# Second block's latent-only adaLN vectors: from TensorE chunks to GpSimd products and ScalarE sums

## The chip, the cores and the metric

One core of one Trainium2 chip runs the whole program in one launch. The metric is the device time in microseconds (us) of that launch; less is better. Engines are named as the profile names them: PE is TensorE's matmuls, DVE is VectorE, ACT is ScalarE, POOL is GpSimd, SP is the queue that issues most transfers. Line numbers (L169) are those of the kernel before; where a line of the changed kernel is meant, the text says so.

## What is computed

Two blocks of a flow-matching backbone, for 256 context tokens and 256 latent tokens of width 1024, and a final norm. Cut to what the change touches:

```python
for layer in range(2):
    mod_l = silu(c) @ mod_w[layer] + mod_b[layer]        # c: (1, 1024), mod_w[layer]: (1024, 6144)
    mod_c = silu(c_ctx) @ mod_w[layer] + mod_b[layer]
    sh1l, sc1l, g1l, sh2l, sc2l, g2l = split(mod_l, 6)   # vectors of 1024
    sh1c, sc1c, g1c, sh2c, sc2c, g2c = split(mod_c, 6)
    # mixer on rmsnorm(x, g) * (1 + sc1) + sh1, added to x with gate g1
    # feed-forward on rmsnorm(x, g') * (1 + sc2) + sh2, added to x with gate g2
    # in the last layer the context takes part in the mixer's input alone
```

So of the second block's six vectors the context needs only the first two (sh1, sc1); the other four (g1, sh2, sc2, g2) are needed for the latent tokens alone.

## The kernel before

The stages follow each other: first block's mixer, first feed-forward (`conv_ffn` with l = 0, 512 tokens), second mixer, second feed-forward (l = 1, 256 tokens). Activations lie transposed, features on partitions. Every large product is made of three matmuls of split operands (L180 to L182): a weight block is copied by ACT into a rounded upper part `wh` (L168), and the rest `wl` = raw - `wh` is made by DVE or POOL (L169). A `Stream` does that: `load` (L154) fetches 16 blocks of 128x128, `split` makes one unit of 8 blocks (128x1024), `get` splits one unit ahead, and a load may also call one function of a list `fill`. `wh` and `wl` have four buffers each, the fetched `raw` two.

The first feed-forward: eleven column pairs j in a first half, eleven in a second. For each pair two products of eight blocks with 512 columns (24 matmuls each, into banks `gps` and `mps`), ACT scales the result (`y`, L823), DVE adds the eight other taps of the convolution (L829), ACT applies silu (L890), POOL multiplies (L893), ACT rounds (`mh`, L896) and POOL makes the rest (`ml`, L897). The up-weights' `wl` are POOL's; each pair uses one load, so two units. The first four products (units of loads 0 and 1) run together. After the eleven pairs come 88 blocks of the down-weights (`dn`), whose first units are POOL's too.

`mod_chunk(l, j)` computes 512 entries of `mod_l` and `mod_c`: two transfers of 1 MB, eight matmuls of 512 columns (L239) with silu(c) as a 128x32 operand, a copy by ACT (L256), four transposes (L259), a sum and bias by DVE (L263 to L267) into `mod` columns (`comps`). Of the second block's twelve chunks, chunk 2 stands ahead of the first feed-forward's norm, nine (3, 0, 1, 4, 5, 8, 9, 6, 7) are its `fill`, one at each load from the third on, chunk 10 stands ahead of the second feed-forward's norm and chunk 11 is its `fill`.

Ahead of each feed-forward stands a norm: `Norm.add(k)` squares the k-th of eight tiles of x on ACT (L281), adds on DVE (L283), sums over partitions on PE (L127), takes the root on DVE (L112 to L118), spreads it by PE and ACT (L135, L136 `rstd`); then `norm_mod` makes `hh` and `hl` for each k on DVE and ACT (L310, L316, L318).

A scheduler orders every engine's instructions when the program is built: it moves an instruction forward where its engine is free and its inputs are there by its own estimate, so what stands late in the code can run early. On the chip each engine then works through its list in that order.

Of the kernel before, what the change touches and what calls it, by code (L numbers as in the profile page):

```python
# [9 lines left out]
F32 = mybir.dt.float32  # L10
F32R = mybir.dt.float32r
I32 = mybir.dt.int32
AF = mybir.ActivationFunctionType
ALU = mybir.AluOpType
AX = mybir.AxisListType

P = 128
D = 1024
KD = 8
# [8 lines left out]
FF = 22  # L28
# [23 lines left out]
def block_kernel(ctx: ExitStack, tc: tile.TileContext, A: dict, out: bass.AP):  # L52
    nc = tc.nc
    PSUM = bass.MemoryType.PSUM
    v, s, g, te = nc.vector, nc.scalar, nc.gpsimd, nc.tensor
# [8 lines left out]
    rawp = ctx.enter_context(tc.tile_pool(name="rawp", bufs=2))  # L64
# [9 lines left out]
    def nm(b):  # L74
        _u[0] += 1
        return f"{b}_{_u[0]}"
# [10 lines left out]
    def mps():  # L87
        return psm.tile([P, 512], F32, tag="m", name=nm("mps"))
# [12 lines left out]
    def pc(name, i=0, n=1):  # L101
        o = _off[name] + i
        return prm[:, o:o + n]
# [124 lines left out]
    comps = [[cp.tile([P, KD, 2], F32, tag=f"mod{l}_{i}", name=f"mod{l}_{i}") for i in range(6)] for l in range(2)]  # L228

    def mod_chunk(l, j, pool=rawp, psa=vps, tag="raw", n=2, bufs=None):  # L230

        ps = psa()
        w = KD // n
        for i in range(n):
            raw = pool.tile([P, w * 512], F32, tag=tag, name=nm("rawm"), bufs=bufs)
            nc.sync.dma_start(out=raw, in_=A["modw"][l, j, :, i * w * 512:(i + 1) * w * 512])
            for kk in range(w):
                k = i * w + kk
                te.matmul(out=ps[32 * (k % 4):32 * (k % 4) + 32, :], lhsT=spad[:, k, :], rhs=raw[:, kk * 512:(kk + 1) * 512],  # L239
                          start=k < 4, stop=k >= 4)  # L240
        mod_out(l, 4 * j, 4, ps, psa)
# [11 lines left out]
    def mod_out(l, c, n, ps, psa):  # L253

        ev = t2((P, n * P))
        s.copy(out=ev, in_=ps)  # L256
        pt = psa()[:, :n * P].rearrange("p (a b) -> p a b", b=P)
        for a in range(n):
            te.transpose(pt[:, a, :], ev[:, a * P:(a + 1) * P], ident)  # L259
        col = lambda name, o: pc(name, o, n).unsqueeze(2).to_broadcast([P, n, 2])  # L260
        i, k = c // KD, c % KD
        dst = comps[l][i][:, k:k + n, :]
        v.tensor_reduce(out=dst, in_=pt.rearrange("p a (q c) -> p a c q", q=4)[:, :, 0:2, :], axis=AX.X, op=ALU.add)  # L263
        v.tensor_tensor(out=dst, in0=dst, in1=col("modb", l * 48 + c), op=ALU.add)
        if i in (1, 4):

            v.scalar_tensor_tensor(out=dst, in0=dst, scalar=1.0, in1=col("nmg" if i == 1 else "nfg", l * 8 + k), op0=ALU.add, op1=ALU.mult)  # L267

    accs = np_.tile([P, T], F32, tag="acc", name="acc", bufs=1)

    class Norm:
# [29 lines left out]
    def norm_mod(l, comp_sh, comp_sc, segs, r, between=lambda k, acts: None, tiles=None):  # L301
        c0, c1 = segs[0][1], segs[-1][2]
        hs = [] if tiles is None else tiles
        sh, sc = comps[l][comp_sh], comps[l][comp_sc]
        acts = lambda k: hs[k]
        for k in range(KD):
            between(k, acts)
            y = t2()
            for ci, a, b in segs:
                v.scalar_tensor_tensor(out=y[:, a:b], in0=xT[k][:, a:b], scalar=sc[:, k, ci:ci + 1], in1=r[:, a - c0:b - c0],  # L310
                                       op0=ALU.mult, op1=ALU.mult)
            if tiles is None:
                hs.append(htiles(k))
            h_, l_ = hs[k]
            for ci, a, b in segs:
                s.activation(out=h_[:, a:b], in_=y[:, a:b], func=AF.Identity, bias=sh[:, k, ci:ci + 1])  # L316
            for ci, a, b in segs:
                v.scalar_tensor_tensor(out=l_[:, a:b], in0=y[:, a:b], scalar=sh[:, k, ci:ci + 1], in1=h_[:, a:b].bitcast(F32),  # L318
                                       op0=ALU.add, op1=ALU.subtract)
        return acts  # L320

    def htiles(k):
        return (hp.tile([P, T], F32R, tag=f"hh{k}", name=nm("hh")), hp.tile([P, T], F32R, tag=f"hl{k}", name=nm("hl")))
# [15 lines left out]
    E = Ctx()  # L339
# [11 lines left out]
    with tc.tile_pool(name="stp", bufs=6) as stp:  # L351
# [19 lines left out]

        acts = norm_mod(0, 0, 1, SEGS, r, start)
    fill0 = [lambda j=j: mod_chunk(0, j) for j in (4, 5, 8, 9, 6, 7)]
    fill1 = [lambda j=j: mod_chunk(1, j) for j in (3, 0, 1, 4, 5, 8, 9, 6, 7, 11)]
    E.fill0, E.W0 = fill0, W0
    nrm = Norm(0, T)
    with ExitStack() as st:
# [4 lines left out]
    mod_chunk(1, 2, rawp, mps)  # L382
    acts = norm_mod(0, 3, 4, SEGS, r)
    with ExitStack() as st:
        hs, nrms = [], [Norm(a, b) for _, a, b in SEGS]

        def then(m, sgs):
            for sg in sgs:
                nrms[sg[0]].add(m)
                if m == KD - 1:  # L390
                    hs[:] = hs or [htiles(k) for k in range(KD)]
                    norm_mod(1, 0, 1, (sg,), nrms[sg[0]].row(), tiles=hs)

        conv_ffn(E, st, 0, acts, fill1[:-1], then)
    for k in range(KD):
        dump(f"x2_{k}", xT[k])
    with ExitStack() as st:
# [3 lines left out]
        dump(f"x3_{k}", xT[k])  # L401
    with ExitStack() as st:
        r = nrm.row()
        mod_chunk(1, 10, rawp, mps)
        acts = norm_mod(1, 3, 4, SEGS[1:], r)
        op = st.enter_context(tc.tile_pool(name="outp", bufs=1))
        ot = op.tile([P, 2, D], F32, tag="ot", name="ot")

        def turn(k):

            y = op.tile([P, TL], F32, tag="yt", name=nm("yt"), bufs=2)
            s.activation(out=y, in_=xT[k][:, 256:T], func=AF.Copy, scale=pc("fng", k))
            pt = mps()
            for t in range(2):
                te.transpose(pt[:, t * P:(t + 1) * P], y[:, t * P:(t + 1) * P], ident)
            s.copy(out=ot[:, :, k * P:(k + 1) * P], in_=pt[:, :TL].rearrange("p (t n) -> p t n", n=P))

        nrm = Norm(256, T)

        def then(m, sgs):  # L420
            nrm.add(m)
            if 0 < m < KD - 1:
                turn(m - 1)

        conv_ffn(E, st, 1, acts, fill1[-1:], then)

        r = nrm.cols()
        turn(KD - 2)
        turn(KD - 1)
        for h in range(2):  # L430
            for t in range(2):
                y = ot[:, t, h * 512:(h + 1) * 512]
                if h == 0:
                    v.tensor_scalar(out=y, in0=y, scalar1=r[:, t:t + 1], scalar2=None, op0=ALU.mult)
                else:
                    s.activation(out=y, in_=y, func=AF.Copy, scale=r[:, t:t + 1])
                nc.sync.dma_start(out=out[t, :, h * 512:(h + 1) * 512], in_=y)
# [364 lines left out]
        then(m)  # L802


def conv_ffn(E, st, l, acts, fill, then):
    nc, tc, A = E.nc, E.tc, E.A
    v, s, g = E.v, E.s, E.g
    nm = E.nm
    full = l == 0
    n = T if full else TL  # L810
# [53 lines left out]

    nh = 2 if full else 1
    per = FF // nh
    dn = E.Stream(A[f"dn{l}"], FF * KD, eng=lambda u: g if u * 8 % (per * KD) < per * 4 else v)
    LAG = 4
    for hf in range(nh):
        hm = []  # L870
# [5 lines left out]
        for jj in range(per):  # L876
            j = hf * per + jj
# [312 lines left out]
def layout(inp):  # L1190
    f = {k: np.asarray(a) for k, a in inp.items()}
    A = {}
    xx = np.concatenate([f["ctx"][0], f["x"][0]], 0)
    A["x"] = xx.T.reshape(KD, P, T).transpose(1, 0, 2).reshape(P, KD * T)
    A["cv"] = np.stack([f["c_ctx"], f["c"][0]], -1).reshape(KD, P, 2).transpose(1, 0, 2).reshape(P, 16)
    A["mods"] = f["mod_w"][0][:, :2048].reshape(KD, P, 8, 256).transpose(2, 1, 0, 3).reshape(8, P, 2048)
    A["modw"] = f["mod_w"].reshape(2, KD, P, 12, 512).transpose(0, 3, 2, 1, 4).reshape(2, 12, P, 4096)
    prm = np.zeros((P, NPRM), np.float32)
# [33 lines left out]
    w = f["even_w_in"][0]  # L1232
# [19 lines left out]
    for l in range(2):  # L1252
# [3 lines left out]
        dn = f["ffn_w_down"][l]  # L1256
# [7 lines left out]
    w = f["ssd_w_in"][0]  # L1264
    z, xs, b, c, dt = np.split(w, np.cumsum([2048, 2048, 512, 512]), axis=1)
# [12 lines left out]
    i = np.arange(P)  # L1278
# [27 lines left out]
```

## Time and profile before

| | us |
|---|---|
| median of three runs | 1296.32 |
| fastest of three runs | 1293.79 |
| third run | 2431.66 |
| profiled execution, its own time | 1291.57 |
| its span in the trace | 1289.4 |

The third run lies far off the others and off the profiled execution. The trace is of one execution on one core; a row of its timeline gives the start and the length in us, the engine, the line, the operation, what it writes and reads, and in brackets how long the engine had been idle and what ended that. Between the span and the execution's time lie 2.2 us.

### The profile page before, as it was taken

How to read it: one execution, taken by the hardware profiler on the slowest of the kernel's cores; microseconds unless marked ns; L12 is line 12 of the kernel's file. 1: busy time of each engine (PE TensorE's matmuls, PEld its weight loads, DVE VectorE, ACT ScalarE, POOL GpSimd, SP SyncE). 2: the span in 40 equal slices, each digit the busy share in tenths (PEclk: the TensorE clock that was granted, in tenths of full speed). 3: DMA queues.
4: the chain of work that ended last, by engine and by line, in shares of the span. 5: the costliest groups of instructions: out<-in, count | busy, mean ns of one | idle time of the engine just before them, and what ended most of it. 6: DMA issues, size and time to landing. Idle time of an engine off the chain costs nothing.

```text
span 1289.4 us, 19329 instructions
## 1 busy us (share of the span) xinstructions
PE 1233.4 (96%) x7358; PEld 1016.6 (79%) x7358; DVE 942.9 (73%) x2137; ACT 596.9 (46%) x947; POOL 385.3 (30%) x214
## 2 busy tenths in 40 slices
PE   7989999999999999999999999999999999899997
PEld 5657787876867677888888897887888888899997
DVE  5483899576658766227774478879888958999993
ACT  4463344343345434124443356656566545555553
POOL 0100000000225555226665000032232125778720
PEclk9989999999999999999999999999999999999999
DMA  9546303324436563222211225444454464545431
GB/s 374 207 173 229 116 16 103 118 91 164 171 145 247 220 262 139 98 98 98 99 66 67 98 76 164 156 140 153 126 152 111 169 243 150 200 165 183 142 131 66
DMA packets 39964, 190.96 MB, mean 148 GB/s; under 512 B 4592, under 2 KB 10552, under 8 KB 20928
## 3 DMA queue, kind: packets, MB, share of 16 engines
q1 hardware_dynamic: 36512, 185.48, 41.2%
q10 hardware_dynamic: 3360, 4.25, 1.1%
q8 instruction: 58, 0.95, 0.3%
q14 instruction: 34, 0.28, 0.1%
HBM read 188.51 MB, written 1.20 MB: 147 GB/s over the span
## 4 chain that ended last, share of the span: by engine, by line
PE 70%; DVE 19%; issue 4%; ACT 3%; DMA 3%; POOL 1%; SPq 0%; ACTq 0%; DVEq 0%; POOLq 0%
PE gps L180 13%; PE gps L181 13%; PE gps L182 13%; DVE y L829 6%; PE mps L180 5%; PE mps L182 4%; PE mps L181 4%; PE vps L239 3%; DVE ml L897 2%; PE vps L1113 1%; PE gps L215 1%; PE gps L216 1%; PE gps L217 1%; DVE y L893 1%; PE vps L1100 1%
## 5 line engine op out<-in xcount | busy, mean ns | idle before, releaser
L169 POOL TENSOR_TENSOR wl<-raw,wh 128x1024 fp32r<-128x1024 f32 x111 | 268.1, 2425 | 514.7 <-ACT wh L168 514.5
L168 ACT ACTIVATE wh<-raw 128x1024 fp32r<-128x1024 f32 x226 | 237.6, 1054 | 170.8 <-PE gps L182 108.4
L180 PE MATMUL gps<-hh,wh 128*128 128x512 f32 (+1 forms) x840 | 296.7, 354 | 7.1 <-ACT hh L316 5.4
L182 PE MATMUL gps<-hl,wh 128*128 128x512 f32 (+1 forms) x840 | 294.8, 352 | 1.6 <-DVE hl L318 1.6
L181 PE MATMUL gps<-hh,wl 128*128 128x512 f32 (+1 forms) x840 | 294.9, 351 | 1.2 <-DVE wl L169 1.1
L829 DVE SCALAR_TENSOR_TENSOR y<-mps,fcw,y 128x255 f32<-128x255 f32 (+3 forms) x576 | 223.1, 427 | 37.3 <-ACT y L823 31.0
L169 DVE TENSOR_TENSOR wl<-raw,wh 128x1024 fp32r<-128x1024 f32 x115 | 140.9, 1232 | 79.5 <-ACT wh L168 79.3
L180 PEld LDWEIGHTS gps<-hh,wh 128*128 128x128 f32 x840 | 159.2, 190 | 43.1 <-issue 11.7
L180 PE MATMUL mps<-hh,wh 128*128 128x256 f32 (+1 forms) x528 | 172.1, 326 | 10.8 <-DVE y L829 8.5
L182 PEld LDWEIGHTS gps<-hl,wh 128*128 128x128 f32 x840 | 159.5, 190 | 25.0 <-issue 4.2
L181 PEld LDWEIGHTS gps<-hh,wl 128*128 128x128 f32 x840 | 159.9, 190 | 24.1 <-issue 4.1
L181 PE MATMUL mps<-hh,wl 128*128 128x256 f32 (+1 forms) x528 | 170.6, 323 | 0.0
L182 PE MATMUL mps<-hl,wh 128*128 128x256 f32 (+1 forms) x528 | 170.6, 323 | 0.0
L180 PEld LDWEIGHTS mps<-hh,wh 128*128 128x128 f32 x528 | 100.3, 190 | 27.6 <-issue 9.3
L180 PE MATMUL gps<-mh,wh 128*128 128x256 f32 (+1 forms) x352 | 117.6, 334 | 2.7 <-ACT mh L896 2.7
L181 PE MATMUL gps<-mh,wl 128*128 128x256 f32 (+1 forms) x352 | 117.2, 333 | 0.0
L182 PE MATMUL gps<-ml,wh 128*128 128x256 f32 (+1 forms) x352 | 117.0, 333 | 0.0
L182 PEld LDWEIGHTS mps<-hl,wh 128*128 128x128 f32 x528 | 100.4, 190 | 7.5
L181 PEld LDWEIGHTS mps<-hh,wl 128*128 128x128 f32 x528 | 100.4, 190 | 7.1
L829 DVE SCALAR_TENSOR_TENSOR y<-gps,fcw,y 128x189 f32<-128x189 f32 (+3 forms) x196 | 83.3, 437 | 23.1 <-ACT y L823 19.3
L823 ACT ACTIVATE y<-mps,fcw 128x256 f32<-128x256 f32 (+1 forms) x66 | 40.6, 639 | 87.7 <-PE mps L182 87.7
L180 PEld LDWEIGHTS gps<-mh,wh 128*128 128x128 f32 x352 | 66.8, 190 | 10.0 <-ACT mh L896 2.9
(281 smaller groups left out, 1836.8 us busy)
## 6 DMA issues: line engine op xcount, KB each, us to landing
raw<-in_up SPq DMA_DIRECT2D x42, 1024.0 KB, 4.9
rawm<-in_modw SPq DMA_DIRECT2D x36, 1024.0 KB, 5.8
raw<-in_win SPq DMA_DIRECT2D x32, 1024.0 KB, 5.3
raw<-in_dn SPq DMA_DIRECT2D x20, 1024.0 KB, 4.9
raw<-in_wout SPq DMA_DIRECT2D x10, 1024.0 KB, 5.0
rawm<-in_mods SPq DMA_DIRECT2D x8, 1024.0 KB, 14.0
R<-crd SPq DMA_DIRECT2D x32, 256.0 KB, 4.3
rawm<-in_modw SPq DMA_DIRECT2D x8, 512.0 KB, 5.1
```

Of the source, the lines that this page charges most:

```text
L168: s.activation(out=hi[:, :n], in_=rw, func=AF.Copy)
L169: self.eng(u).tensor_tensor(out=lo[:, :n], in0=rw, in1=hi[:, :n].bitcast(F32), op=ALU.subtract)
L180: te.matmul(out=ps, lhsT=lhi, rhs=rhi, start=first, stop=False)
L181: te.matmul(out=ps, lhsT=llo, rhs=rhi, start=False, stop=False)
L182: te.matmul(out=ps, lhsT=lhi, rhs=rlo, start=False, stop=last)
L215: te.matmul(out=ps, lhsT=ah[:, sl], rhs=hi[:, c:c + 512], start=k == 0, stop=False)
L216: te.matmul(out=ps, lhsT=ah[:, sl], rhs=lo[:, c:c + 512], start=False, stop=False)
L217: te.matmul(out=ps, lhsT=al[:, sl], rhs=hi[:, c:c + 512], start=False, stop=k == nk - 1)
L239: te.matmul(out=ps[32 * (k % 4):32 * (k % 4) + 32, :], lhsT=spad[:, k, :], rhs=raw[:, kk * 512:(kk + 1) * 512], start=k < 4, stop=k >= 4)
L823: s.activation(out=y, in_=ps, func=AF.Identity, scale=fcw[:, ti * 10 + 4:ti * 10 + 5], bias=fcw[:, ti * 10 + 9:ti * 10 + 10])
L829: v.scalar_tensor_tensor(out=o, in0=i, scalar=fcw[:, ti * 10 + wi:ti * 10 + wi + 1], in1=o, op0=ALU.mult, op1=ALU.add)
L897: part = lambda ya=ya, h_=h_, l_=l_: ep.tensor_tensor(out=l_, in0=ya, in1=h_.bitcast(F32), op=ALU.subtract)
```

## The change

The chunks 4 to 11 of the second block, those of the four latent-only vectors, are no longer computed by PE. Their 4096 columns of `mod_w` are stored transposed, as 32 tiles of 128x1024 (512 KB, the same bytes as before). For each tile a 128x1024 row of silu(c), the same on all partitions, is multiplied in on POOL, and ACT copies the product and sums it along the row into one `mod` column. Two `wt` buffers hold the tiles. `take(n)` finishes the tiles fetched by the last call and fetches n more; it is called at the up-weights' loads (14 tiles) and at the down-weights' loads (18 tiles) of the first feed-forward. The chunks 3, 0 and 1 stay as they were.

```diff
+    class Rows:
+        def __init__(self, pool):
+            self.pool, self.c, self.ready = pool, 0, []
+            self.row = pool.tile([P, D], F32, tag="row", name="row")
+            nc.sync.dma_start(out=self.row, in_=A["crow"].to_broadcast([P, D]))
+            th = pool.tile([P, D], F32, tag="wt", name=nm("wt"), bufs=2)
+            s.activation(out=th, in_=self.row, func=AF.Tanh, scale=0.5)
+            g.tensor_scalar(out=th, in0=th, scalar1=0.5, scalar2=0.5, op0=ALU.mult, op1=ALU.add)
+            g.tensor_tensor(out=self.row, in0=self.row, in1=th, op=ALU.mult)
+        def take(self, n):
+            for c, w in self.ready:
+                i, k = 2 + c // KD, c % KD
+                dst = comps[1][i]
+                g.tensor_tensor(out=w, in0=w, in1=self.row, op=ALU.mult)
+                s.activation(out=w, in_=w, func=AF.Copy, accum_out=dst[:, k, 1:2])
+                if k == KD - 1:
+                    d = dst[:, :, 1]
+                    v.tensor_tensor(out=d, in0=d, in1=pc("modb", 48 + 8 * i, 8), op=ALU.add)
...
+            self.ready = []
+            for _ in range(n):
+                w = self.pool.tile([P, D], F32, tag="wt", name=nm("wt"), bufs=2)
+                nc.sync.dma_start(out=w, in_=A["modt"][self.c])
+                self.ready.append((self.c, w))
+                self.c += 1
...
-    fill1 = [lambda j=j: mod_chunk(1, j) for j in (3, 0, 1, 4, 5, 8, 9, 6, 7, 11)]
+    fill1 = [lambda j=j: mod_chunk(1, j) for j in (3, 0, 1)]
...
+        rows = Rows(st.enter_context(tc.tile_pool(name="mw", bufs=1)))
+        def behind(i):
+            if i < 3:
+                fill1[i]()
+            rows.take(1 if i % 3 < 2 else 0)
+        upf = [lambda i=i: behind(i) for i in range(20)]
+        dnf = [lambda n=n: rows.take(n) for n in [2] * 9 + [0] * 2]
...
-        conv_ffn(E, st, 0, acts, fill1[:-1], then)
+        conv_ffn(E, st, 0, acts, upf, then, dnf)
...
-        mod_chunk(1, 10, rawp, mps)
...
-        conv_ffn(E, st, 1, acts, fill1[-1:], then)
+        conv_ffn(E, st, 1, acts, None, then)
...
+    A["crow"] = f["c"].reshape(1, D)
+    A["modt"] = f["mod_w"][1][:, 2048:].T.reshape(32, P, D)
```

The first place is POOL's list in the first half of the first feed-forward, at the two units of the loads 7 and 8. `wl` of `raw` are the weights' lower parts, `y` and `ml` the two POOL steps of a column pair, `wt` the new tiles. Before:

```order
L169 TENSOR_TENSOR wl_3855<-raw_3829,wh_3854 128x1024
L897 TENSOR_TENSOR ml_3797<-y_3659,mh_3796 128x512
L169 TENSOR_TENSOR wl_3914<-raw_3829,wh_3913 128x1024
L893 TENSOR_TENSOR y_3771<-y_3771,y_3769 128x512
L169 TENSOR_TENSOR wl_3968<-raw_3942,wh_3967 128x1024
L897 TENSOR_TENSOR ml_3910<-y_3771,mh_3909 128x512
L169 TENSOR_TENSOR wl_4027<-raw_3942,wh_4026 128x1024
```

In the changed kernel the same stretch reads (L287 is the product of a tile with the row, L934 and L938 are L893 and L897):

```order
L169 TENSOR_TENSOR wl_3813<-raw_3808,wh_3812 128x1024
L938 TENSOR_TENSOR ml_3776<-y_3656,mh_3775 128x512
L287 TENSOR_TENSOR wt_4857<-wt_4857,row 128x1024
L287 TENSOR_TENSOR wt_4951<-wt_4951,row 128x1024
L169 TENSOR_TENSOR wl_3872<-raw_3808,wh_3871 128x1024
L287 TENSOR_TENSOR wt_5135<-wt_5135,row 128x1024
L934 TENSOR_TENSOR y_3750<-y_3750,y_3748 128x512
L169 TENSOR_TENSOR wl_3905<-raw_3900,wh_3904 128x1024
L938 TENSOR_TENSOR ml_3868<-y_3750,mh_3867 128x512
L287 TENSOR_TENSOR wt_5229<-wt_5229,row 128x1024
L287 TENSOR_TENSOR wt_5415<-wt_5415,row 128x1024
L169 TENSOR_TENSOR wl_3964<-raw_3900,wh_3963 128x1024
```

Between `wl` and `wl` now stand up to two products. The tiles wt_4857 to wt_5415 belong, in the code, to the second half; all 32 products stand in POOL's list ahead of the second half's first pair, the last of them just ahead of the first unit of the down-weights: 7 ahead of the `wl` of load 2, and 25 between that one and the first of the down-weights, among 20 `wl`, 9 `y` and 9 `ml`.

The second place is ACT's list ahead of the first feed-forward, around the last square of the norm (t_558, of the eighth tile x_95) and `rstd`. Before:

```order
L281 ACTIVATE t_552_2960<-x_93 128x512
L168 ACTIVATE wh_3209<-raw_3207 128x1024
L281 ACTIVATE t_556_2994<-x_94 128x512
L168 ACTIVATE wh_3237<-raw_3207 128x1024
L281 ACTIVATE t_558_3024<-x_95 128x512
L256 COPY t_569_3075<-mps_3062 128x512
L136 COPY rstd_3040<-vps_3056 128x512
```

In the changed kernel (L288 is the copy that sums a tile into a `mod` column, L313 is L281):

```order
L313 ACTIVATE t_552_2960<-x_93 128x512
L288 ACTIVATE wt_3624,mod_2_114<-wt_3624 128x1024
L288 ACTIVATE wt_3718,mod_2_114<-wt_3718 128x1024
L168 ACTIVATE wh_3218<-raw_3216 128x1024
L313 ACTIVATE t_556_2994<-x_94 128x512
L288 ACTIVATE wt_3902,mod_2_114<-wt_3902 128x1024
L168 ACTIVATE wh_3246<-raw_3216 128x1024
L288 ACTIVATE wt_3996,mod_2_114<-wt_3996 128x1024
L313 ACTIVATE t_558_3024<-x_95 128x512
L256 COPY t_569_3075<-mps_3062 128x512
L288 ACTIVATE wt_4180,mod_2_114<-wt_4180 128x1024
L136 COPY rstd_3040<-vps_3056 128x512
```

Six sums (two of them above this piece) now stand ahead of the last square, and a seventh ahead of `rstd`. On POOL the products of these tiles stand between the `wl` of the loads 0 and 1, on SP their transfers between those of the weights.

## Rows read from the trace of the kernel before

**Rows 1.** Page, part 1: busy us, share of the span, instructions.
```profile
PE 1233.4 (96%) x7358; PEld 1016.6 (79%) x7358; DVE 942.9 (73%) x2137; ACT 596.9 (46%) x947; POOL 385.3 (30%) x214
```
**Rows 2.** Stretches: length, busy us of each engine, PE clock, DMA share, GB/s.
```profile
371.90:501.60 129.70, 129.70 (x651) 94.64 (x650) 91.73 (x229) 53.38 (x75) 71.15 (x38) 1.00 0.59 219
580.00:602.00 22.00, 22.00 (x99) 18.22 (x98) 17.52 (x42) 8.99 (x12) 13.97 (x8) 1.00 0.27 96
```
**Rows 3.** Timeline of ACT, first feed-forward, first and second half.
```profile
435.51 0.78 ACT L823 ACTIVATE y<-gps,fcw 128x512 f32<-128x512 f32 x1 [3.71 <-PE gps L182]
...
448.97 0.78 ACT L823 ACTIVATE y<-gps,fcw 128x512 f32<-128x512 f32 x1 [3.71 <-PE gps L182]
...
608.19 0.78 ACT L823 ACTIVATE y<-gps,fcw 128x512 f32<-128x512 f32 x1 [3.19 <-PE gps L182]
...
619.07 0.78 ACT L823 ACTIVATE y<-gps,fcw 128x512 f32<-128x512 f32 x1 [3.19 <-PE gps L182]
```
**Rows 4.** Groups by line, 325 to 510 us: count, busy us, mean ns, idle before.
```profile
L169 POOL TENSOR_TENSOR wl<-raw,wh 128x1024 fp32r<-128x1024 f32 x25 | 60.2, 2406 | 355.2 <-ACT wh L168 355.1
...
L168 ACT ACTIVATE wh<-raw 128x1024 fp32r<-128x1024 f32 x28 | 29.4, 1051 | 20.3 <-PE gps L182 7.8 <-issue 7.8 <-POOL wl L169 2.8
...
L897 POOL TENSOR_TENSOR ml<-y,mh 128x512 fp32r<-128x512 f32 x10 | 13.0, 1302 | 2.2 <-ACT mh L896 2.2
L893 POOL TENSOR_TENSOR y<-y,y 128x512 f32<-128x512 f32 x10 | 12.9, 1294 | 14.0 <-DVE y L829 14.0
```
**Rows 5.** Timeline of POOL: `wl` of loads 0 and 2, and of the first down-weights.
```profile
339.45 2.42 POOL L169 TENSOR_TENSOR wl<-raw,wh 128x1024 fp32r<-128x1024 f32 x1 [288.42 <-ACT wh L168]
...
371.90 2.41 POOL L169 TENSOR_TENSOR wl<-raw,wh 128x1024 fp32r<-128x1024 f32 x1 [13.77 <-ACT wh L168]
...
499.17 2.40 POOL L169 TENSOR_TENSOR wl<-raw,wh 128x1024 fp32r<-128x1024 f32 x1 [4.35 <-ACT wh L168]
```
**Rows 6.** Timeline of ACT: the norm's last square, and `rstd`.
```profile
355.60 0.61 ACT L281 ACTIVATE t<-x 128x512 f32<-128x512 f32 x1
...
361.22 0.59 ACT L136 COPY rstd<-vps 128x512 f32<-128x512 f32 x1 [1.18 <-PE vps L135]
```
**Rows 7.** Timeline of PE: first up-product, first down-product of the first half.
```profile
363.32 0.50 PE L180 MATMUL gps<-hh,wh 128*128 128x512 f32 x1 [2.13 <-ACT hh L316]
...
508.05 0.40 PE L180 MATMUL gps<-mh,wh 128*128 128x512 f32 x1
```
**Rows 8.** Timeline: one DVE operation alone, and again while POOL is busy.
```profile
385.25 0.17 DVE L264 TENSOR_TENSOR mod<-mod,c 128x8 f32<-128x8 f32 x1
...
399.28 2.41 POOL L169 TENSOR_TENSOR wl<-raw,wh 128x1024 fp32r<-128x1024 f32 x1
399.60 2.11 DVE L264 TENSOR_TENSOR mod<-mod,c 128x8 f32<-128x8 f32 x1
```
**Rows 9.** Page, part 6: transfers of 512 KB, count, median us to landing.
```profile
rawm<-in_modw SPq DMA_DIRECT2D x8, 512.0 KB, 5.1
...
raw<-in_win SPq DMA_DIRECT2D x6, 512.0 KB, 3.5
...
raw<-in_up SPq DMA_DIRECT2D x4, 512.0 KB, 7.4
```
**Rows 10.** Timeline of PE after an idle time; a stretch, columns as in rows 2.
```profile
85.47 1.94 PE L239 MATMUL vps<-rawm,spad 128*32 128x512 f32 x8 [2.88 <-DVE mod L263]
...
85.00:92.00 7.00, 6.53 (x20) 3.90 (x21) 6.94 (x16) 2.97 (x5) 0.00 (x0) 0.52 0.49 156
```
**Rows 11.** Timeline ahead of the second feed-forward: DVE's root, chunk 10's sum, chunk 11.
```profile
1061.34 0.16 DVE L116 TENSOR_TENSOR rw<-ry 128x2 f32<-128x2 f32 x1
1062.01 0.19 DVE L263 TENSOR_REDUCE mod<-mps 128x8 f32<-128x32 f32 x1 [0.50 <-PE mps L259]
...
1064.07 1.53 PE L239 MATMUL vps<-rawm,spad 128*32 128x512 f32 x2 [0.46 <-ACT rstd L136]
```

More of the change, by code (lines that the diff above doesn't have):

```diff
@@ L267, in mod_out @@
             v.scalar_tensor_tensor(out=dst, in0=dst, scalar=1.0, in1=col("nmg" if i == 1 else "nfg", l * 8 + k), op0=ALU.add, op1=ALU.mult)
+    class Rows:
[16 more added lines that the diff above has]
+                    v.tensor_tensor(out=d, in0=d, in1=pc("modb", 48 + 8 * i, 8), op=ALU.add)
+                    if i == 4:
+                        v.scalar_tensor_tensor(out=d, in0=d, scalar=1.0, in1=pc("nfg", 8, 8), op0=ALU.add, op1=ALU.mult)
+            self.ready = []
[4 more added lines that the diff above has]
+                self.c += 1
     accs = np_.tile([P, T], F32, tag="acc", name="acc", bufs=1)
@@ L802, in even_mixer, with conv_ffn @@
         then(m)
-def conv_ffn(E, st, l, acts, fill, then):
+def conv_ffn(E, st, l, acts, fill, then, dfill=None):
     nc, tc, A = E.nc, E.tc, E.A
@@ L866, in conv_ffn @@
     per = FF // nh
-    dn = E.Stream(A[f"dn{l}"], FF * KD, eng=lambda u: g if u * 8 % (per * KD) < per * 4 else v)
+    dn = E.Stream(A[f"dn{l}"], FF * KD, dfill, eng=lambda u: g if u * 8 % (per * KD) < per * 4 else v)
     LAG = 4
```

## Prediction

> **What bounds the kernel now.** I read the page's shares first [rows 1]: PE is busy for 96% of the span, POOL for 30%. That invites work to move from PE to POOL, but the shares are means over the program, so the second view is the table of stretches around the change [rows 2]. In the first half of the first feed-forward, from the `wl` of load 2 to shortly past that of the first down-weights, PE is busy for 129.70 of 129.70 us at full clock and POOL for 71.15: it has 58.6 us free there. In the second half PE is full too. The third view is the timeline of ACT's `y` [rows 3]: two neighbouring pairs with a chunk stand 448.97 - 435.51 = 13.46 us apart, two without 619.07 - 608.19 = 10.88. So a chunk costs 2.58 us on PE, and what leaves PE is gained until something else is late. What can be late is POOL: every `wl` of the up-weights and of the first down-weights is its work, and PE's three matmuls per block need it. The fourth view gives POOL's prices [rows 4]: `wl` 2406 ns, `y` 1294 and `ml` 1302.
>
> **What goes.** Eight chunks: six beside the column pairs of the first feed-forward, worth 6 x 2.58 = 15.5 us of PE, and chunks 10 and 11 (term D). The bytes fetched are the same: 32 tiles of 512 KB for eight chunks of 2 MB.
>
> **What comes.** 32 products of 128x1024. No row has this operation alone, but `wl` has the same size and two f32 SBUF inputs, and subtracting takes as long per column as multiplying (`y` 1294, `ml` 1302 for 512 columns [rows 4]). So I take 2.41 us each: below, two of the 512-column products would be 2.59, above, so the size is narrow; 32 x 2.41 = 77 us on POOL. The two operations that make the row run while POOL is idle, 288 us ahead of its first `wl` [rows 5]. ACT gets 32 sums. A copy of the shape, `wh`, takes 1.05 [rows 4]; what the accumulator's write adds no row shows. Bounds: 1.05, and 2.1 as for a second pass; I take 1.2, near the row. ACT is busy for 53 of 130 us [rows 2], so 25 x 1.2 = 30 us fit, but they stand in order in its list, which is what matters below. The additions on DVE are a few small ones of 0.17 us, or 2.1 beside POOL.
>
> POOL's list in the front part is what decides. All 32 products stand ahead of the second half: 7 ahead of the `wl` of load 2, 25 from there to the `wl` of the first down-weights, where 20 `wl`, 9 `y` and 9 `ml` stand already.
>
> **Term A, the norm ahead of the feed-forward.** ACT's last square ran at 355.60 [rows 6]; now sums stand ahead of it, and each waits for its product, which waits on POOL behind the `wl` of loads 0 and 1. With two `wt` buffers a transfer goes out only when a sum has freed one, and lands 3.5 to 7.4 us later [rows 9]. Walking the queues from POOL's first `wl` at 339.45 [rows 5] (m is a product): `wl` to 341.9, m 344.3, m 347.4 (waited for its transfer), `wl` 349.8, m 352.4, its sum 353.7, `wh` 354.7, `wl` 357.2, m 359.6, m 362.0, sum 363.2. So the square starts at about 363.2, 7.6 us late. `rstd`, at 361.22 before [rows 6], comes at about 369.6, since the root's operations run beside POOL, and with it the first up-product (363.32 [rows 7]). A = +8; without any wait in this walk it would be +4.4, and with a transfer more to wait for +13.
>
> DVE's share in this: the same 128x8 addition took 0.17 us alone and 2.11 where it began 0.32 after a `wl` on POOL, ending with it (401.71 and 401.69) [rows 8]. So a DVE operation with two SBUF inputs waits for the end of the POOL operation that runs. With POOL nearly always busy such waits become the rule: `norm_mod`'s operations, the root's passes and the sums of the down-product. For `norm_mod` I put 4.1 us, the delay of the `wh` behind the last `hl`; it is in term B.
> The Trainium skill (SBUF — State Buffer, section "Who interferes with whom") states it as a rule: GpSimd and the second ports of VectorE are one pair with an exclusive lock, and a VectorE instruction with two SBUF inputs contends with a GpSimd instruction that reads SBUF; rows 8 agree. The same rule says that one with a single SBUF input is free, by which the column pairs' taps that read PSUM would go on undisturbed; the sum would then stand as given, and by the lock on every DVE operation it would be higher.
>
> **Term B, POOL feeds the products.** The `wl` of load 2 moves from 371.90 to 379.9 with term A. From there to the end of the first down-weights' `wl` POOL had 20 x 2.41 + 18 x 1.30 = 71.6 us of work; it gets 25 x 2.41 = 60.3 more, 131.9. That alone fills its time: 379.9 + 131.9 = 511.8 without a single wait. But its list is strictly in order, and I find waits in it by walking it against ACT's:
> - at the start 4.1, as above;
> - in ten places the `wh` on ACT stands behind a sum whose product POOL has only just ended: sum 1.2, then the centre's scaling 0.78 and `wh` 1.05, some 3 us in which POOL has one other operation of 1.3 to 2.4. Summed over the ten, 17.1;
> - in four places `y` or `ml` waits for ACT, 3.6 together;
> - two tiles have not landed, 2.4.
>
> Together 27 us. The first down-weights' `wl` ends at 511.8 + 27.2 = 539.0; before, PE started there at 508.05 [rows 7], after a `wl` that ended at 501.57 [rows 5]. PE itself would be ready at about 371.3 + (508.05 - 363.32) - 15.5 = 500.5, so it waits. B with A in it is 539.0 - 508.05 = +30.9. What is late next: nothing. No product is left, the second half [rows 3] and the second mixer run as before, and the loss is not made up, since PE is full there [rows 2]. Bounds: no wait +3.8; each of the ten waits at twice the size +48.
>
> **Term C, the clock.** PE now pauses in each pair and for some 8 us ahead of the down-products. After an idle time of 2.88 us the trace shows a stretch of 7 us at a mean granted clock of 0.52, about the 1.2 GHz level, before it is full again [rows 10]. One such costs up to 7 x 0.48 = 3.4 us. Most fall in time that PE waits anyway; I take +2 at the down-products (0 to 3.4). That the whole half runs at the low level is a rival.
>
> **Term D, chunks 10 and 11.** Ahead of the second feed-forward DVE runs chunk 10's sum between the root and `rstd`, and PE has chunk 11 (two matmuls at 1.53) ahead of its first product [rows 11]. I take -2; bounds 0 (all hidden) and -5 (two whole chunks' PE time).
>
> **The sum.** 30.9 + 2 - 2 = +30.9 on the profiled 1291.57: 1322.5. The profiled run is the fastest known; of the runs shown two are undisturbed, 1293.79 and the median 1296.32, and the three average 1293.9. I forecast 1293.9 + 31 = 1325 us.
>
> **Rivals.**
> 1. POOL's idle time holds the products and PE stays the bound: 1294 - 15.5 - 2 = 1277, faster, by under 2%. For: POOL's 58.6 us free against 60.3 of products, so on the sum of work it misses by little. Against: it needs PE's 115 us (129.7 less six chunks) to hold 71.2 + 25 products, so one under 1.76 us, with no waits; rows 4 show 2.41. Chance 0.07.
> 2. POOL is the bound, but the chip keeps its list full: +3.8 - 2, about 1296, no change. For: ACT has room and the waits I sum are small pieces, each of which would vanish if ACT were 2 us ahead. Against: a two-buffer ring of tiles ties POOL, ACT and the transfers together. Chance 0.16.
> 3. The forecast, 1325 (1303 to 1345): chance 0.65.
> 4. PE's pauses of some 3 us in every pair drop its clock to the lower level for the half, as in rows 10; a product of 24 matmuls (5.4 us, half a pair) would take 10.9, two of them 21.8 against a POOL pair of about 14. PE would then be the bound again from the point at which half of the pairs run low: 5 x 7 = 35 us at the worst on top of 1325, 1345 to 1375, slower. For: the pauses are as long as that of rows 10. Against: one pair keeps PE busy for 10 us in between. Chance 0.12.
>
> **How the numbers follow.** A range of 1300 to 1350 leaves out rival 1, half of rival 2 and most of rival 4, about 0.2. A change of 2% is 25.9 us, about what a measurement of this kernel can tell from no change. The forecast's own range, 1303 to 1345, lies for two thirds beyond 1319.8: slower 0.43 + 0.12 = 0.55; within 2% the other 0.22, rival 2 and most of rival 1: 0.42; faster 0.03.
>
> **What would show it.** Right: POOL busy without gaps to speak of from about 380 to 540; ACT's last square near 363 behind a sum; pairs some 14 us apart in the first half, with PE idle ahead of matmuls that wait for `wl`; the first down-product near 539; the second half's pairs 10.88 apart as before; the second feed-forward 2 us earlier. Wrong: products under 2 us; the first down-product ahead of 515; sums much over 1.2 us on ACT, by which ACT would be the bound; a PE clock near 0.5 in the half.

## The result and the profile after

The changed kernel takes 1327.91 us in the median of four runs (1326.04 to 1331.22), the kernel before 1295.78 beside it. The ratio is 1.0264, 95% interval 1.0243 to 1.0286: slower by 2.6%. The ratio leaves out the one run before of 2431.66 and is therefore not the quotient of the two medians. The forecast was 1325, slower.

The page's first line and two stretches (columns as in [rows 2]) of the kernel after:

```profile
PE 1224.0 (92%) x7198; PEld 1017.4 (77%) x7198; DVE 952.9 (72%) x2124; ACT 627.5 (47%) x1004; POOL 464.1 (35%) x248
...
371.90:501.60 129.70, 113.34 (x491) 86.31 (x492) 87.12 (x193) 63.37 (x101) 96.44 (x48) 0.93 0.53 191
381.87:539.04 157.17, 128.42 (x552) 98.93 (x550) 98.68 (x219) 77.24 (x121) 129.22 (x63) 0.93 0.47 171
```

In the stretch of [rows 2] PE was busy for 129.70 us and is now busy for 113.34: it waits. The second row goes from POOL's `wl` of load 2 to the end of the first down-weights' one. POOL works for 129.22 of 157.17 us there and waits for the other 27.95. The timeline of ACT, PE and POOL has the events of [rows 5 to 7]:

```profile
363.83 0.61 ACT L313 ACTIVATE t<-x 128x512 f32<-128x512 f32 x1
371.49 0.58 ACT L136 COPY rstd<-vps 128x512 f32<-128x512 f32 x1 [2.29 <-PE vps L135]
373.99 0.80 PE L180 MATMUL gps<-hh,wh 128*128 128x512 f32 x1
381.87 2.42 POOL L169 TENSOR_TENSOR wl<-raw,wh 128x1024 fp32r<-128x1024 f32 x1 [13.85 <-issue]
...
536.68 2.36 POOL L169 TENSOR_TENSOR wl<-raw,wh 128x1024 fp32r<-128x1024 f32 x1 [0.52 <-ACT wh L168]
539.10 0.50 PE L181 MATMUL gps<-mh,wl 128*128 128x512 f32 x1 [1.95 <-POOL wl L169]
...
608.00 0.78 ACT L864 ACTIVATE y<-gps,fcw 128x512 f32<-128x512 f32 x1 [4.40 <-PE gps L182]
618.88 0.78 ACT L864 ACTIVATE y<-gps,fcw 128x512 f32<-128x512 f32 x1 [3.19 <-PE gps L182]
```

The first up-product stands 10.67 us later than before, the first down-product that needs a POOL `wl` 30.82 (539.10, before 508.28). After that the distance hardly grows: the second half's pairs are 10.88 apart again. Groups of 335 to 545 us show who waited for whom:

```profile
L287 POOL TENSOR_TENSOR wt<-wt,row 128x1024 f32<-128x1024 f32 x32 | 77.8, 2443 | 5.0 <-DMA wt<-in_modt 4.9
...
L288 ACT ACTIVATE wt<-wt 128x1024 f32<-128x1024 f32 x32 | 33.8, 1057 | 70.0 <-POOL wt L287 70.0
```

A product takes 2.44 us. The 32 sums take 34 us of ACT, but ACT stands idle for 70.0 us ahead of them: 24 of the 32 wait for their product. That row became the key. PE's own waits from the `wl` of load 2 to 539.10 point the same way:

```profile
PE vps L259 <- ACT t L256: 10.5, 3, 6.6
PE mps L180 <- DVE y L870: 9.6, 2, 6.9
PE gps L181 <- POOL wl L169: 3.8, 2, 1.9
PE mps L181 <- POOL wl L169: 3.4, 2, 2.5
```

Only 7.2 of some 28.7 us of idle time end with a `wl`. Nearly all the rest ends with a remaining chunk's copy `t` on ACT, or with DVE's taps, which wait for ACT's `y`; on ACT the long ones of both stand behind a sum.

### The profile page after: what moved, and what is told of

The parts are those of the page before. It is cut to its first block, busy times and chain, and to the rows that moved or that the text cites. A ratio compares the mean times of both kernels' runs of the same rounds, so it can differ in the third digit from the quotient of the medians.

```text
span 1324.3 us, 19147 instructions
## 1 busy us (share of the span) xinstructions
PE 1224.0 (92%) x7198; PEld 1017.4 (77%) x7198; DVE 952.9 (72%) x2124; ACT 627.5 (47%) x1004; POOL 464.1 (35%) x248
## 4 chain that ended last, share of the span: by engine, by line
PE 37%; DVE 17%; POOL 7%; issue 4%; ACT 4%; DMA 1%; ACTq 0%; SPq 0%; POOLq 0%
DVE y L870 9%; PE gps L180 9%; PE gps L181 9%; PE gps L182 9%; POOL wt L287 3%; POOL wl L169 2%; DVE ml L938 2%; PE mps L180 2%; PE mps L181 2%; PE mps L182 2%; DVE y L934 1%; PE vps L1154 1%; ACT wh L168 1%; PE vps L1141 1%; PE mps L1107 1%
## 5 line engine op out<-in xcount | busy, mean ns | idle before, releaser
L287 POOL TENSOR_TENSOR wt<-wt,row 128x1024 f32<-128x1024 f32 x32 | 77.8, 2443 | 5.0 <-DMA wt<-in_modt 4.9
```

Of the source, the lines that this page charges most:

```text
L287: g.tensor_tensor(out=w, in0=w, in1=self.row, op=ALU.mult)
```

## The experiments

Times are medians, or one time where one run was made; a ratio is a kernel's time over that of the kernel before, whose median is 1293 to 1295 beside all of them. "First down-product" is PE's first of the first half: 508.05 before, 536.65 after.

### Products held at their place in the code

```diff
+                with tc.issue_after(held[0]):   # POOL's last wl in the code
+                    g.tensor_tensor(out=w, in0=w, in1=self.row, op=ALU.mult)
```

> Same work as the change, but every product is held on POOL behind the last wl that stands ahead of it in the code, so the scheduler cannot bring it forward: some 8 products in the first half's pairs instead of 25. Theory (POOL's in-order list is the bound of the first half): POOL then has about 71.6 + 8 x 2.4 = 91 us of work there, under PE's 115, PE is the bound again and the six chunks are gained: 1294 - 15.5 + 3 (clock and second feed-forward) = about 1281 (1276 to 1290), the first down-product near 498 to 503. Rival (the products cost as much wherever they stand, because they hold DVE and ACT): over 1305.

1308.55, ratio 1.0106 (1.0075 to 1.0138). The first down-product came at 499.09, as expected, but the time is in the rival's range: the first half's down-products, which took from 508.05 to 570.06 before, took from 499.09 to 572.91, 11.8 us longer, and the second half's took 11.8 us longer too. ACT waited 109.4 us for products in all. So the products' place was more than half of the loss (1.0264 to 1.0106), and the sums still stopped ACT.

### Short products, short sums

Each product, or each sum, works on `w[:, :64]`.

> The change with each product cut to 64 of 1024 columns (most of the dot product is left out); transfers, sums and their waits stay. Theory (POOL's work is what is late): the first down-product comes near 500 and the time is about 1283. Rival (the 32 full sums on ACT, in its list ahead of wh, or the two-buffer ring of tiles): still over 1305.

1297.96, first down-product 512.34. Products of 0.35 us, and still 20 us later than the removed chunks allow: `rstd` came 8.1 late, the sums waited 45.9 us, and ACT's `y<-gps` came 12.9 us apart (460.44, 473.36, 486.28), where a pair is 10.88 on PE. A stretch and two rows of PE:

```profile
460.44:486.28 25.84, 25.84 (x116) 21.40 (x115) 17.71 (x41) 15.35 (x27) 17.05 (x15) 1.00 0.57 204
...
498.71 0.77 PE L180 MATMUL mps<-hh,wh 128*128 128x512 f32 x1 [5.04 <-DVE y L870]
499.28 0.63 PE L181 MATMUL mps<-hh,wl 128*128 128x512 f32 x1
```

PE is full there and runs ahead of ACT; later it stands idle for 5.04 us until DVE's taps end. Neither theory foresaw this.

> The change with each sum cut to 64 of 1024 columns (most of the sum is left out); products and transfers stay whole. Theory (POOL's work bounds, the sums only add waits): POOL's 131.9 us in the first half stay, of its 28 us of waits those ten in which wh stands behind a sum shrink by some 0.9 each: first down-product near 526 to 532, time about 1315. Rival (ACT's sums are the bound): about 1283.

1328.08, first down-product 541.35: a miss. Shorter sums brought nothing; they waited 76.1 us. But the scheduler had put the products earlier still, and POOL ran nearly without a gap from 446 to 520, so this run does not price the sums' length by itself.

### The kernel before without chunks 10 and 11

> The kernel before with chunks 10 and 11 left out (the last gate vector is a constant, set once), nothing added. As forecast (DVE's root and PE are freed): 2 us faster than before, 1292. Theory formed from the trace after (PE idles longer ahead of the second feed-forward's first products and runs them at the lower clock): 1 to 3 us slower than before, PE's granted clock near 0.5 for 10 us there.

Ratio 1.0012 (0.9998 to 1.0026): 1.5 us slower by the middle, and the gain of 2 is out. PE's timeline and two stretches of this run, the first of them the 5 us from the first up-product:

```profile
1062.00 0.66 PE L135 MATMUL vps<-c,ry 128*128 128x128 f32 x2 [3.68 <-DVE ry L118]
1064.18 0.58 PE L180 MATMUL gps<-hh,wh 128*128 128x256 f32 x1 [1.52 <-ACT hh L318]
...
1064.18:1069.18 5.00, 5.00 (x23) 5.00 (x24) 4.55 (x12) 2.05 (x5) 0.00 (x0) 0.50 0.00 0
...
1250.00:1260.00 10.00, 8.60 (x49) 8.47 (x50) 6.23 (x13) 5.71 (x15) 0.00 (x0) 0.66 0.29 106
```

The same places of the kernel before:

```profile
1063.20 0.41 PE L135 MATMUL vps<-c,ry 128*128 128x128 f32 x2 [1.23 <-DVE ry L118]
...
1065.53 0.58 PE L180 MATMUL gps<-hh,wh 128*128 128x256 f32 x1
...
1065.53:1070.53 5.00, 5.00 (x34) 5.00 (x34) 4.15 (x11) 2.40 (x5) 0.00 (x0) 0.76 0.49 205
...
1250.00:1260.00 10.00, 9.05 (x62) 8.93 (x63) 6.36 (x13) 7.33 (x18) 0.00 (x0) 0.83 0.25 98
```

With chunk 10 gone PE idles 3.68 us ahead of the norm's spread, where it idled 1.23, and its clock at the first up-products is 0.50, the 1.2 GHz level, where it was 0.76. `rstd` is on time and the first products are slow: from this `rstd` to the first `y` of the second feed-forward it is 12.35 us, before 10.87.

### What the chunks are worth, and products without sums

> The change with its 32 products and 32 sums left out (the four vectors are constants, set once); its 32 transfers and the missing chunks stay. It shows what the removal of the eight chunks alone is worth. If the wait for tiles or the transfers themselves cost anything: over 1290. If they are hidden, as all theories but the one on the two-buffer ring say: PE is the bound, the first down-product near 493 (508.05 - 15.5) and the time about 1294 - 15.5 + 1.5 (second feed-forward at the lower clock) = 1280.

1284.15. From `rstd` to the first down-product 131.33 us, before 146.83: the 15.5 is exact. This run's `rstd` was 3.2 late, which is most of what the time misses 1280 by.

> The change with all sums left out (constant vectors), products and transfers whole. Theory (POOL's list is the bound, and a good part of its 28 us of waits comes from the sums that stand ahead of wh and y on ACT): POOL runs with few waits, its 132 us of work set the time, the first down-product comes near 510 to 522, the time is 1296 to 1308. If POOL's own work alone explains the loss: first down-product over 532, time over 1318. If the sums alone explain it: near 493 and 1280.

1317.88: a miss, between the two ends, and for a reason of its own. DVE's root of the norm ran beside POOL's products and `wl`:

```profile
361.11 1.19 DVE L112 TENSOR_SCALAR rm<-most 128x4 f32<-128x4 f32 x1
362.34 2.27 DVE L113 TENSOR_SCALAR rw<-rm 128x4 int32<-128x4 int32 x1
364.64 2.26 DVE L114 TENSOR_SCALAR ry<-rw 128x4 int32<-128x4 int32 x1
...
371.52 2.26 DVE L118 SCALAR_TENSOR_TENSOR ry<-rw,ry 128x4 f32<-128x4 f32 x1
373.82 0.16 DVE L116 TENSOR_TENSOR rw<-ry 128x4 f32<-128x4 f32 x1
```

Five operations of four columns take 2.26 us each instead of 0.17, `rstd` comes at 376.23, 15 late. From there to the first down-product it is 153.2 us, against 165.2 in the changed kernel and 131.3 without POOL's work. So by these three runs some 12 of the 34 us lost there hang on the sums and 22 on products bunched in front of the down-weights. It is an estimate: the lists differ a little (23 products stand in this stretch here, 25 in the changed kernel), and each of the three was profiled once.

### Fewer products, one per pair

Products are held as in the first run. The call in the up-weights' loads, for 16 tiles and for 8; the down-weights' loads fetch none, and the other chunks return to PE.

```diff
-            rows.take(1 if i % 3 < 2 else 0)
+            rows.take(1 if i in (4, 5, 6, 7, 8, 9, 10, 11, 12, 13, 14, 15, 16, 17, 18, 19) else 0)    # second run: 11 to 18
```

> Only four chunks (4 to 7) become products, 16 tiles; chunks 8 and 9 go back to PE in the first half, 10 and 11 to the second feed-forward. One product per pair, held behind the last wl of the code: 5 in the first half after its chunk pairs, 11 in the second half, none among the down-weights. POOL has 4.8 + 2.6 + 2.4 = 9.8 us of work in such a pair of 10.88. Theory (products are cheap only where POOL has room in each pair): 4 x 2.58 = 10.3 gained, some 0.3 lost per product: 1286 to 1290, faster than before. Rival (any product in a pair costs its 2.4 us): over 1300.

1305.00, ratio 1.0081 (1.0059 to 1.0103).

> Only two chunks (4 and 5) become products, 8 tiles, all in the pairs of the second half, one per pair; the other chunks are as before. Theory: 2 x 2.58 = 5.2 gained, under 1.5 lost: 1290. Rival (any product in a pair costs its 2.4 us): 8 x 2.4 - 5.2 = 14 slower, 1308.

1300.69, ratio 1.0040 (1.0026 to 1.0054). Both miss: on average a product costs some 1.3 us, though POOL has room. One round in the run with eight, timeline of ACT, DVE and POOL (L871 is the centre, L877 the taps, L941 `y`, L293 the product, L294 the sum):

```profile
629.88 0.77 ACT L871 ACTIVATE y<-mps,fcw 128x512 f32<-128x512 f32 x1
630.75 4.61 DVE L877 SCALAR_TENSOR_TENSOR y<-mps,fcw,y 128x255 f32<-128x255 f32 x10 [3.60 <-ACT y L871]
635.50 1.29 POOL L941 TENSOR_TENSOR y<-y,y 128x512 f32<-128x512 f32 x1 [1.44 <-DVE y L877]
636.75 2.42 POOL L172 TENSOR_TENSOR wl<-raw,wh 128x1024 fp32r<-128x1024 f32 x1
639.11 2.41 POOL L293 TENSOR_TENSOR wt<-wt,row 128x1024 f32<-128x1024 f32 x1
641.55 1.06 ACT L294 ACTIVATE wt<-wt 128x1024 f32<-128x1024 f32 x1 [4.09 <-POOL wt L293]
642.61 0.76 ACT L871 ACTIVATE y<-mps,fcw 128x512 f32<-128x512 f32 x1
```

This is a ring: the centre waits on ACT behind the sum, the sum for its product, the product on POOL behind `wl` and `y`, `y` for DVE's taps, the taps for the centre before. 0.87 + 4.75 + 1.25 + 2.36 + 2.44 + 1.06 = 12.73 us a round, PE's pair is 10.88, and no engine is full. The sum takes the place of PE as the thing that the centre waits for.

### The ring cut: sums one call later

A third tile buffer, and each sum is issued at the next call, behind the last `wh` on ACT:

```diff
+            for c, w in self.done:
+                with tc.issue_after(heldA[0]):      # ACT's last wh
+                    s.activation(out=w, in_=w, func=AF.Copy, accum_out=dst[:, k, 1:2])
...
             for c, w in self.ready:
                 g.tensor_tensor(out=w, in0=w, in1=self.row, op=ALU.mult)
-                s.activation(out=w, in_=w, func=AF.Copy, accum_out=dst[:, k, 1:2])
...
+            self.done, self.ready = self.ready, []
```

> As the run with sixteen tiles in the pairs, with one difference: each sum is held on ACT until one load later, behind a wh (three tile buffers instead of two), so that when ACT comes to it its product has long ended. Theory formed from that run (a ring: ACT's centre stands behind the sum, the sum waits for its product, the product stands on POOL behind a wl and y, y waits for DVE's taps, the taps for the centre before; 12.7 us a round, with no engine full): the ring is cut, pairs of the second half go back to 10.88, 10.3 us are gained: 1284 to 1288. Rival (POOL's 2.4 us per product cost PE that time wherever the sum stands): pairs still at 12.7 and 1305.

1284.48, ratio 0.9927 (0.9906 to 0.9947), where the same 16 tiles gave 1.0081. The same places in this run (L873 centre, L301 product, L293 sum):

```profile
612.75 1.05 ACT L293 ACTIVATE wt<-wt 128x1024 f32<-128x1024 f32 x1
614.80 2.38 POOL L301 TENSOR_TENSOR wt<-wt,row 128x1024 f32<-128x1024 f32 x1
616.04 0.78 ACT L873 ACTIVATE y<-mps,fcw 128x512 f32<-128x512 f32 x1 [2.15 <-PE mps L187]
...
625.66 2.40 POOL L301 TENSOR_TENSOR wt<-wt,row 128x1024 f32<-128x1024 f32 x1
626.92 0.78 ACT L873 ACTIVATE y<-mps,fcw 128x512 f32<-128x512 f32 x1 [2.15 <-PE mps L187]
```

The centre waits for PE, no longer for a sum; rounds are 10.88 with the product in them. The third buffer is not what did it: in the run with the same sixteen tiles no product waited for its tile.

> The same with 24 tiles: the six chunks 4 to 9 become products, one per load of up-weights from the sixth on and seven among the loads of the down-weights; only 10 and 11 stay on PE, in the second feed-forward. Theory: another 5.2 us gained in the pairs, 0 to 4 given back among the down-weights: 1279 to 1286. Rival: over 1305.

1278.22, ratio 0.9877 (0.9857 to 0.9898): faster than both kernels, and in front by some 50 us of the changed one. First down-product 496.01. Its groups:

```profile
L301 POOL TENSOR_TENSOR wt<-wt,row 128x1024 f32<-128x1024 f32 x24 | 57.7, 2405 | 1.9 <-DMA wt<-in_modt 1.9
...
L293 ACT ACTIVATE wt<-wt 128x1024 f32<-128x1024 f32 x24 | 25.2, 1048 | 0.0
```

58 us of products cost PE next to nothing: some 15.3 us are gained where six chunks are worth 15.5. No sum waits.

> The change with all its 32 tiles and its calls, with one difference: each sum is held on ACT to the next call, behind a wh, with a third tile buffer. The products are not held, but since tiles come free later they spread by themselves. If the order of sums and products is the cause of the whole loss and the amount of POOL's work is not: PE is the bound again, the first down-product near 497, and the time is 1279 to 1287. If the amount of POOL's work (77 us) in the first feed-forward costs by itself: over 1300.

1282.09, ratio 0.9906 (0.9891 to 0.9921): the change itself, all 32 tiles, no product held. The stretch of [rows 2] in this run:

```profile
371.90:501.60 129.70, 128.57 (x593) 101.84 (x592) 97.20 (x237) 63.37 (x91) 93.96 (x49) 1.00 0.42 158
```

PE is full again. Six products stand in the first half's pairs instead of 25, since a tile now comes free only after the later sum; so this one edit both cuts the ring and spreads the products, and the run doesn't part the two; the first run, which spread them and left the sums, stayed at 1.0106. ACT still waited 9.8 us ahead of sums.

> As the run with 24 tiles and late sums, but with all 32 (chunks 10 and 11 too leave PE; one product per load of up-weights from the first on, twelve among the down-weights). If the removal of chunks 10 and 11 gains what was forecast: 2 us faster than with 24, 1276. If PE's longer pause and its lower clock ahead of the second feed-forward take that back: 1 to 3 us slower, 1279 to 1281, a granted clock near 0.5 there.

1281.56, ratio 0.9894 (0.9876 to 0.9913): some 2 us more than with 24 tiles, but the intervals of the two overlap. PE's pause is there (3.69 us, a clock of 0.59 in the 5 us around it), but in the two traces the `rstd` ahead of the second feed-forward is already 1.65 us later with 32 tiles, and from it to the first `y` only 0.26 us are added. So this pair says little of the chunks.

## Why the prediction was right, step by step

- **The norm late (A).** Forecast square 363.2, `rstd` 369.6, `wl` of load 2 379.9; measured 363.83, 371.49, 381.87. The 2 us more lie in the transfers and in one operation of the root, which took 2.15 us beside a product on POOL.
- **POOL feeds the products (B).** Forecast 131.9 us of work and 27.2 of waits, down-products from 539.0; measured 129.22, 27.95 and 539.10. The kinds agree too: for `wh` 21.2 forecast (4.1 + 17.1) and 21.2 measured (18.9 and 2.3 that the waits view files under issue), for `y` and `ml` 3.6 against 4.5, for tiles 2.4 against 2.2. The price of a product, taken from `wl` at 2.41, was 2.44; a sum held ACT for 1.06 to 1.15, taken 1.2. That the end agrees to 0.1 us is luck: the start was 2.0 late and the work 2.7 short. Where PE waits is not as forecast: it was to be ready at 500.5 and to wait for `wl`, in pairs 14 us apart. The pairs' `y<-gps` came 16 us apart on average (416.51 to 512.76), the up-products ended at 535.57, PE paused 3 us instead of 8 ahead of the down-products, and three quarters of its idle time came by way of ACT's list, as the waits above show.
- **The clock (C).** +2 forecast; from the first down-products to the second half's first `y` the delay grew from 30.82 to 32.45 (608.00 against 575.55 in the trace of before), 1.6, with a granted clock of 0.83 from 539 to 549 us.
- **Chunks 10 and 11 (D).** This step failed: -2 forecast. The second feed-forward's first `y` is 33.71 late and the end 34.9, so +1.3 and another +1.2. Two stretches of the kernel after, at the second feed-forward's first products and at the last down-products, and one near the end of the run with sixteen late sums, which keeps chunks 10 and 11:

```profile
1098.00:1103.00 5.00, 5.00 (x26) 5.00 (x25) 3.83 (x10) 1.33 (x4) 0.00 (x0) 0.50 0.00 0
...
1284.00:1294.00 10.00, 9.36 (x55) 9.23 (x56) 5.43 (x12) 6.44 (x15) 0.00 (x0) 0.66 0.24 95
...
1244.00:1254.00 10.00, 9.72 (x61) 9.59 (x62) 5.84 (x12) 6.97 (x18) 0.00 (x0) 0.72 0.21 88
```

Five us of products at the 1.2 GHz level after a pause of 3.69: the run without chunks 10 and 11 shows this with nothing else changed, and all traces here part by it. From that `rstd` to the first `y` it is 11.24 to 12.43 us in the nine without the two chunks (pause 3.68 or 3.69) and 10.87 to 10.98 in the five with them (pause 1.23 or 1.24). The time that was forecast is gained, since the first up-product comes 0.7 us earlier than the delay of 32.45, and the slow products take 2.0 back. So the step counted the chunks' time and not what their matmuls did for what follows them: they had kept PE busy through the norm. The +1.2 at the end is not theirs as far as shown. A slow stretch there (0.66, before 0.83) comes with the chunks too (0.72), and the change with late sums, which leaves them out, runs the same place at 1.00; why it comes and goes stays open.
- **The sum.** 30.8 + 1.6 + 1.3 + 1.2 = 34.9 in the span, against 30.9.
- **Rivals.** PE's clock in the half was 0.93, not near 0.5, so the fourth fell. The second (a full list without waits) fell with the 27.95 us. The first asked for a product under 1.76 us, for 25 products in the first half; with late sums a product still takes 2.4 us and PE is full, but six to eleven stand there and nearly all others behind, so 25 with late sums were not tried. POOL's idle time does hold the products, if they are spread and no sum stands ahead of a centre.

So the arithmetic was right for this order of instructions, and the reason only in part: POOL's bunched products are the larger share of the loss, as forecast, but the prediction counted the sums' waits one by one and did not see that they close a ring that sets a pace of its own. Four of the expectations above were missed by it: for sixteen and eight tiles the rows show the ring, for held and for short products only the sums' waits.

## What to carry to other kernels

Work moved to an idle engine is priced by the lists it joins: ask which instruction on a second engine waits for it, and what stands behind that one. A consumer that is issued right behind its producer on another engine turns the producer's delay into a stop; one round later, with one more buffer, the same work was all but free here. And a matmul group that shortens a pause may be worth more than its time.

## What was not expected of the hardware

- DVE operations of four columns, TENSOR_SCALAR with one SBUF input among them, took 2.26 us beside POOL's 1024-column products and `wl`, and 0.17 without. The Trainium skill (SBUF — State Buffer, section "Who interferes with whom") names tensor_scalar among the operations that can take the port pair that VectorE shares with GpSimd; this trace agrees. The same section says that an instruction with one SBUF input, outside those two-port modes, does not contend; the prediction left that condition out. That rule is seen in the taps that read PSUM: in the run with eight tiles ten of them take 4.61 us beside a `wl` on POOL, as in the kernel before.
- A ring over three engines, each well under full, set 12.73 us where the busiest needed 10.88.
